# Two triangular inversions, issued as one block or step by step beside TensorE's main stream

## The chip, the cores and the metric

The kernel runs on one NeuronCore of a Trainium2 chip. The metric is the time of one execution on the device, in microseconds (us). Five engines take part: TensorE (PE: matrix products and transposes), VectorE (DVE), ScalarE (ACT), GpSimd (POOL) and SyncE (SP), whose queue issues nearly all the transfers of this kernel. Each engine runs its own list of instructions in order; semaphores make one engine wait for another.

## The reference

One step of a small hybrid decoder with an even and an odd layer, for a prompt of 2048 rows and 8 sample rows. The even layer has differential attention (4 heads) and a gated delta rule (4 heads) side by side. The change concerns the delta rule, which works in chunks:

```
M  = where(strict, (kb @ k^T) * decay, 0)
Tm = triangular_solve(eye + M, eye)          # the inverse of a unit lower triangle
u  = Tm @ (v * beta);  w = Tm @ (kb * exp(g))
# then, chunk by chunk, with the state S:
v_new = u - w @ S
o     = qg @ S + attn @ v_new
S     = S * gl + kg^T @ v_new
```

Every chunk of every head needs its `Tm` before the state can pass through it.

## The kernel before

The prompt is worked in two halves of 1024 rows (8 blocks of 128). All matrices of the projections are split into a high and a low part, and each product is made of three (`mm3`, lines 392 to 400).

**The parts of a half.** `a_group` (head by head) projects query, key and value of attention; `b_group` projects the delta rule's inputs, and `stage_a` behind it builds the chunk matrices and stores each chunk's strict triangle `N` in DRAM (`gn_d`); `z_group` projects the gates, `zt`, evacuated by ScalarE (tanh) and VectorE (a fused multiply and add that reads PSUM) from two PSUM buffers (line 508 on). `scan` runs the recurrence over 8 chunks; for each, `merge` reads the inverted diagonal blocks from DRAM (16 small loads a chunk, lines 741 and 742) and puts them together to the inverse of the whole chunk.

**The inversion.** `inverse` (lines 681 to 701) inverts the 32x32 diagonal blocks of all chunks and heads of a half: 128 blocks, one on each partition. It loads them with four transfers (`ivN`, line 687), sets `X` to the unit matrix, and goes over 31 rows, last to first. For a row with m entries right of the diagonal it multiplies (`ivp`, m x m products, `X` read transposed) and sums (`ivX`, a reduction to m values). Each row needs the row before it. In half 0 both instructions are on VectorE; in half 1 the 20 larger products (`r < IP`) are on GpSimd. At the end `X` and its transpose are stored (lines 698 and 701) for `merge`.

**What sets the order.** The Python functions are generators that trace instructions. `drive(main, *sides)` traces the main stream piece by piece, counts the TensorE time of each piece (its columns / 2400 us) on a clock, and traces one step of a side stream (`Side(gen, gap)`) whenever the clock has passed its due time, which then moves on by `gap`. `drain` traces what is left of a side stream; `run` traces a generator to its end. The traced order is not the final one: the kernel is built with `schedule_with_timeline_sim=True` (line 1920), by which a planner lays out each engine's list ahead of time with assumed durations, taking among the instructions whose operands are there by then the one traced first. `after` adds an order between two instructions; a `Side` with a window (`WS0A`, `WT0A`) uses it so that the main stream's products don't get too far ahead of the side's.

**Around the change.** In half 0 the last gates (`zb`, four `z_group` columns) are traced at lines 1720 to 1724, the last of them by `run(zb)`. The next lines traced are those of half 1: first `inverse(gp, 0)` and the first four gate columns of half 0 (lines 1699 and 1700), then `scan` of half 0 as a side stream (line 1701), `build_hT` (the normed input rows of half 1) and `a_group(…, 1, 0)`. In half 1, the first 16 of 64 pieces of `zb` are traced at line 1721; then come `inverse(gp, 1)` (line 1726), the other 48 pieces with attention of half 0 as a side stream `at` (lines 1734 and 1735), `a_group(…, 1, 1)`, and from there on `scan` of half 1 (line 1738) as a second side stream. Attention loads keys (`kl`), values, queries (`ql`) and, at each change of head, a row of biases (`biasR`), which VectorE turns round (`biasT`).

Of the kernel before, what the change touches and what calls it, by code (L numbers as in the profile page):

```python
# [33 lines left out]
SK = 6  # L34
KM = 3
CT = 0
WARM = 16
IP = 20
PC = (0,)
# [75 lines left out]
def hybrid_step_kernel(  # L115
# [209 lines left out]
    def run(*gens):  # L325
        for g in gens:
            for _ in g:
                pass
# [33 lines left out]
    def drive(main, *sides):  # L362
        n, m = len(PE.log), len(DVE.log)
        pace = []
        for t in main:
            clock[0] += t or 0.0
            if len(DVE.log) > m:
                pace.append(DVE.log[-1])
            for s in sides:
                if s.win and len(s.pe) >= s.win:  # L370
                    after(PE.log[n:], s.pe[-s.win])
            for s in sides:
                while not s.done and clock[0] >= s.due:
                    k = len(DVE.log)
                    s.step(pace)
                    if not s.vwin and len(DVE.log) > k:
                        pace.append(DVE.log[-1])
            n, m = len(PE.log), len(DVE.log)
# [139 lines left out]
    def z_group(st, wp, hs, half, idx):  # L518
        ws = [load_cols(wp, wic[i]) for i in idx]
        for part in range(2):  # L520
            for i, w in zip(idx, ws):
                ev = z_evac(st, i, half, part)
                for off, n in PARTS[half][part][2]:
                    ps = psD.tile([P, 512], F32, tag="d", name="psz")
                    yield from mm_cols(ps[:, :n], w, hs, part, off, n)
                    ev(ps[:, :n], off, n)
# [154 lines left out]
    def inverse(gp, half):  # L681
        N = gp.tile([P, 32, 32], F32, tag="pka", bufs=1, name="ivN")
        X = gp.tile([P, 32, 32], F32, tag="pkb", bufs=1, name="ivX")
        pr = gp.tile([P, 1024], F32, tag="ww", bufs=1, name="ivp")
        base = gn_d.offset + half * NB * H * P * P
        for b in range(4):
            SP.dma_start(N[32 * b:32 * b + 32],
                         bass.AP(tensor=gn_d.tensor, offset=base + 32 * b * P + 32 * b,
                                 ap=[[P * P, 32], [P, 32], [1, 32]]))
        DVE.memset(X, 0.0)  # L690
        DVE.memset(X.rearrange("p r c -> p (r c)")[:, ::33], 1.0)
        for r in range(30, -1, -1):
            m = 31 - r
            pv = pr[:, :m * m].rearrange("p (c s) -> p c s", s=m)
            tt(pv, bc(N[:, r:r + 1, r + 1:], [P, m, m]),
               X[:, r + 1:, r + 1:].rearrange("p s c -> p c s"), ALU.mult, POOL if half == 1 and r < IP else None)
            DVE.tensor_reduce(X[:, r, r + 1:], pv, axis=AX.X, op=ALU.add, negate=True)
        SP.dma_start(xb_d[half].rearrange("b u r c -> (b u) (r c)"), X.rearrange("p r c -> p (r c)"))
        prx = pr.rearrange("p (c r) -> p c r", r=32)
        DVE.tensor_copy(prx, X.rearrange("p r c -> p c r"))  # L700
        SP.dma_start(xbt_d[half].rearrange("b u r c -> (b u) (r c)"), pr)
# [977 lines left out]
    with ExitStack() as e1:  # L1679
        wp = (e1.enter_context(tc.tile_pool(name="wp", bufs=4)), 3)  # L1680
        st = e1.enter_context(tc.tile_pool(name="st", bufs=2))
        gsm = e1.enter_context(tc.tile_pool(name="gsm", bufs=2))
        with ExitStack() as eg:
            gp = eg.enter_context(tc.tile_pool(name="gp", bufs=1, side="right"))
            zt = []
            for i in range(6):
                z = gp.tile([P, H, P], F32, tag=f"zt{i}", name=f"zt{i}")
                DVE.memset(z, 0.0)
                zt.append(z)
            S = [gp.tile([P, H, P], F32, tag="S", bufs=2, name="S")]  # L1690
            DVE.memset(S[0], 0.0)
            psG0 = eg.enter_context(ExitStack())
            psG = psG0.enter_context(tc.tile_pool(name="psG0", bufs=3, space=PSUM, side="right"))
            gs = []
            for half in range(2):
                with tc.tile_pool(name=f"bh{half}", bufs=2, side="right") as bp, \
                        tc.tile_pool(name=f"psB{half}", bufs=2, space=PSUM, side="right") as psB:
                    if half == 1:
                        inverse(gp, 0)
                        run(z_group(st, wp, hs, 0, range(0, 2)), z_group(st, wp, hs, 0, range(2, 4)))  # L1700
                        sc = Side(scan(gp, psG, 0, gs[0], S, zt), GS0A, WS0A)
                    hs, build = build_hT(bp, psB, half)
                    ab = gsm.tile([P, NB, 8], F32, tag="ab", name="ab")
                    drive(a_group(st, wp, hs, half, 0, ab, build), *([sc] if half else []))
                with tc.tile_pool(name=f"sa{half}", bufs=1, side="right") as sa, \
                        tc.tile_pool(name=f"psA{half}", bufs=3, space=PSUM, side="right") as psA:
                    g = {}
                    gs.append(g)
                    pend = [gates(sa, psA, half, ab, gsm, g)]
                    sd = [Side(pump(pend), GA)] + ([sc] if half else [])  # L1710
                    if half == 0:
                        for h in range(1, H):
                            drive(a_group(st, wp, hs, half, h, None), *sd)
                    if half == 1:
                        sc.pace(GS0B, WS0B)
                    for h in range(H):
                        drive(b_group(st, wp, sa, psA, hs, half, h, g, pend), *sd)
                    if half == 1:
                        drain(sc)
                    zb = chain(z_group(st, wp, hs, half, range(4, 6)), z_group(st, wp, hs, half, range(6, 8)))  # L1720
                    drive(islice(zb, ZB), *sd)
                    flush(pend)
                    if half == 0:
                        run(zb)
            psG0.close()
            inverse(gp, 1)
            with tc.tile_pool(name="psG1", bufs=2, space=PSUM, side="right") as psG:
                with tc.tile_pool(name="atl0", bufs=1, side="right") as al, \
                        tc.tile_pool(name="atz0", bufs=1, side="right") as az, \
                        tc.tile_pool(name="ate0", bufs=1, side="right") as ae, \  # L1730
                        tc.tile_pool(name="psS0", bufs=2, space=PSUM, side="right") as psS, \
                        tc.tile_pool(name="psX0", bufs=1, space=PSUM, side="right") as psX, \
                        tc.tile_pool(name="psO0", bufs=1, space=PSUM, side="right") as psO:
                    at = Side(attention(split_tags(ae, al, az), psS, psX, psO, psX, "x", 0, 3), GT0A, WT0A)
                    drive(zb, at)
                    at.pace(GT0B, WT0B)
                    drive(a_group(st, wp, hs, 1, 1, None), at)
                    sc = Side(scan(gp, psG, 1, gs[1], S, zt), GS1C, WS1)
                    at.pace(GT0C, WT0C)
                    for h in range(2, H):  # L1740
                        drive(a_group(st, wp, hs, 1, h, None), at, sc)
                    zg = chain(z_group(st, wp, hs, 1, range(0, 2)), z_group(st, wp, hs, 1, range(2, 4)))
                    at.pace(GT0D, WT0D)
                    sc.pace(GS1D, WS1)
                    drive(islice(zg, ZH), at, sc)
                    drain(at, sc)
                SP.dma_start(gdn_p, S[0])
                pr = psG.tile([P, 512], F32, tag="g", name="prh")
                PE.transpose(pr[:36, :P], hist.rearrange("p g j -> p (g j)"), ident)
                hr = gp.tile([36, P], F32, tag="rr", bufs=1, name="hr")  # L1750
                DVE.tensor_copy(hr, pr[:36, :P])
                for gi in range(12):
                    SP.dma_start(gconv_p[0, 0, :, gi * P:gi * P + P], hr[gi * 3:gi * 3 + 3])
            hold(zg, HB0, RB0, at)
# [9 lines left out]
    with ExitStack() as e3, ExitStack() as eS:  # L1764
        wp = (e3.enter_context(tc.tile_pool(name="wp2", bufs=4)), 1)
# [158 lines left out]
```

## Time and profile before

| | |
|---|---|
| median of three runs | 2559.68 us (2556.47 to 2561.66) |
| profiled execution | 2560.37 us, of which the span from the first to the last instruction is 2558.7 |
| mean granted clock of TensorE | 0.981 |
| busy: PE | 2459.0 us (96%) |
| busy: DVE | 1752.6 us (68%) |
| busy: ACT | 1123.4 us (44%) |
| busy: POOL | 785.2 us (31%) |
| chain of work that ended last | PE 74%, DVE 10%, DMA 6%, ACT 3%, issue 3%, POOL 3% |

In rows of instructions the columns are: start, duration, engine, line, operation, output<-inputs, shapes, count, and in brackets the idle time of the engine before it and what ended it. Nearly all instructions have line 131 (the helper that records them), so they are told apart by the names of their tiles. In rows of stretches, busy times and numbers of instructions (x) follow for each engine, then the granted clock of TensorE as a share of full speed, the mean share of the DMA engines and GB/s.

### The profile page before, as it was taken

The numbers are of one execution on the slowest core, as the hardware profiler recorded it, in microseconds if no ns is written. First come the engines' busy times: TensorE is split into PE (matmuls) and PEld (weight loads), VectorE is DVE, ScalarE is ACT, GpSimd is POOL, SyncE is SP. The second block draws the span as 40 slices with busy tenths as digits, with TensorE's granted clock in tenths as the row PEclk, the third lists the DMA queues.
The fourth block names the chain that finished last, engine by engine and source line by source line (L and its number), as shares of the span: only waits on it lengthen the run. The fifth ranks groups of instructions, "written<-read, shape, count | busy, mean of one in ns | idle before, by whom it ended". The sixth has DMA issues, their size and how long they took to land.

```text
span 2558.7 us, 42320 instructions
## 1 busy us (share of the span) xinstructions
PE 2459.0 (96%) x14717; PEld 2164.2 (85%) x14717; DVE 1752.6 (68%) x4133; ACT 1123.4 (44%) x3129; POOL 785.2 (31%) x883
## 2 busy tenths in 40 slices
PE   9999999999998999989899899999999998999998
PEld 8989888988887999878778677788877788999986
DVE  7347766677778677667667878988866457666652
ACT  6445542655544566445543234344444353233220
POOL 3221110211125222101113767644311025555410
PEclk9999999999999999989999999999999999999999
DMA  4334464455453454465334544434354661221252
GB/s 160 112 113 125 127 169 124 131 158 151 140 160 106 122 157 119 122 208 180 109 108 152 171 126 145 149 114 142 114 165 150 214 199 32 75 67 51 73 162 73
DMA packets 262554, 337.45 MB, mean 132 GB/s; under 512 B 62842, under 2 KB 179068, under 8 KB 262332
## 3 DMA queue, kind: packets, MB, share of 16 engines
q1 hardware_dynamic: 252100, 301.18, 38.8%
q0 software_dynamic: 10240, 33.56, 4.5%
q8 instruction: 116, 1.90, 0.3%
q14 instruction: 98, 0.80, 0.1%
HBM read 246.99 MB, written 87.79 MB: 131 GB/s over the span
## 4 chain that ended last, share of the span: by engine, by line
PE 74%; DVE 10%; DMA 6%; ACT 3%; issue 3%; POOL 3%; SPq 0%; ACTq 0%; POOLq 0%; DVEq 0%
PE psp L131 13%; PE psw L131 12%; PE psa L131 10%; PE pso L131 8%; PE psb L131 8%; PE psz L131 4%; PE po L131 4%; PE s L131 3%; PE psy L131 2%; PE px L131 2%; DVE p L131 1%; DVE nm L131 1%; DVE wlo L131 1%; DMA E<-gr_d 1%; DMA wraw<-in_w_out_even_dram 1%
## 5 line engine op out<-in xcount | busy, mean ns | idle before, releaser
L926 ACT ACTIVATE p<-s,nm 128x512 f32<-128x512 f32 (+3 forms) x320 | 199.0, 625 | 293.4 <-DVE nm L131 255.6
L954 POOL TENSOR_SCALAR p<-p,gf 128x512 f32<-128x512 f32 (+3 forms) x160 | 123.0, 782 | 364.6 <-DVE gf L131 221.0
L131 PE MATMUL psp<-whi,ah 128*128 128x512 f32 (+1 forms) x544 | 217.4, 401 | 5.9 <-DVE xres L131 3.0
L131 PE MATMUL pso<-hhi,whi 128*128 128x512 f32 x512 | 208.2, 407 | 2.4 <-DVE ot L131 0.8
L131 PE MATMUL pso<-hhi,wlo 128*128 128x512 f32 x512 | 205.2, 401 | 0.0
L131 PE MATMUL pso<-hlo,whi 128*128 128x512 f32 x512 | 205.1, 401 | 0.0
L131 PE MATMUL psp<-wlo,ah 128*128 128x512 f32 x512 | 204.2, 399 | 0.5 <-DVE wlo L131 0.5
L131 PE MATMUL psp<-whi,al 128*128 128x512 f32 x512 | 203.1, 397 | 0.0
L131 DVE TENSOR_TENSOR wlo<-wraw,whi 128x1024 fp32r<-128x1024 f32 (+2 forms) x128 | 151.3, 1185 | 66.0 <-ACT whi L313 64.2
L313 ACT CAST whi<-wraw 128x1024 fp32r<-128x1024 f32 (+2 forms) x136 | 135.1, 998 | 135.4 <-PE psz L131 29.9
L131 PE MATMUL psa<-whi,hhi 128*128 128x384 f32 (+1 forms) x544 | 190.5, 351 | 1.5 <-ACT hhi L283 1.5
L131 PE MATMUL psa<-wlo,hhi 128*128 128x384 f32 (+1 forms) x544 | 186.2, 342 | 1.4 <-DVE wlo L131 1.3
L131 PE MATMUL psa<-whi,hlo 128*128 128x384 f32 (+1 forms) x544 | 187.3, 344 | 0.0
L131 PE MATMUL psb<-hhi,whi 128*128 128x512 f32 (+1 forms) x480 | 175.9, 367 | 2.4 <-ACT xc L587 2.4
L131 PE MATMUL psb<-hhi,wlo 128*128 128x512 f32 (+1 forms) x480 | 168.7, 352 | 0.0
L131 PE MATMUL psb<-hlo,whi 128*128 128x512 f32 (+1 forms) x480 | 168.0, 350 | 0.0
L131 DVE TENSOR_REDUCE nm<-s 128x1 f32<-128x512 f32 (+3 forms) x256 | 147.3, 587 | 19.7 <-PE s L131 18.4
L131 PE MATMUL po<-v,at 128*128 128x128 f32 x1088 | 157.3, 282 | 0.7 <-ACT at L963 0.7
L131 PEld LDWEIGHTS po<-v,at 128*128 128x128 f32 x1088 | 147.4, 198 | 8.1 <-ACT at L963 1.9
L131 PE MATMUL s<-kst,QH 128*128 128x512 f32 (+3 forms) x320 | 126.4, 406 | 26.8 <-ACT p L926 26.3
L131 DVE SCALAR_TENSOR_TENSOR p<-p,gf 128x512 f32<-128x512 f32 (+3 forms) x160 | 130.8, 840 | 13.7 <-POOL p L954 13.4
L131 DVE TENSOR_TENSOR xres<-xres,psp 128x512 f32<-128x512 f32 (+1 forms) x68 | 46.6, 685 | 123.1 <-PE psp L131 96.8
(413 smaller groups left out, 6923.9 us busy)
## 6 DMA issues: line engine op xcount, KB each, us to landing
wraw<-in_w_in_even_c_dram SPq DMA_DIRECT2D x40, 512.0 KB
asrc<-og_d SPq DMA_DIRECT2D x32, 512.0 KB
wraw<-in_w_in_odd_dram SPq DMA_DIRECT2D x32, 512.0 KB
wr<-in_w_in_odd_dram SPq DMA_DIRECT2D x32, 512.0 KB
wraw<-in_w_in_even_a_dram SPq DMA_DIRECT2D x24, 384.0 KB
xrow<-in_x_prompt_dram SPq DMA_DIRECT2D x16, 512.0 KB
qd_d<-qn SPq DMA_DIRECT2D x64, 128.0 KB
gu_d<-cv SPq DMA_DIRECT2D x32, 256.0 KB
```

What stands on the lines that cost most here:

```text
L131: r = f(*a, **k)
L313: ACT.copy(hi, raw)
L926: ACT.activation(p[:, e, :w], s[:, :w], AF.Exp, bias=nm, accum_out=b["sums"][:, e, c:c + 1])
L954: POOL.tensor_scalar(p[:, 1, :w], p[:, 1, :w], gf[:, 1, c:c + 1], 1.0, ALU.mult, ALU.mult)
```

## The change

`inverse` yields after its setup and after every row. In half 0 it becomes a side stream with a step of 1.3 us of the main stream's clock beside the four gate columns that were traced behind it; what is left is drained before the scan is set up. In half 1 it becomes a side stream with a step of 1.6 us beside the rest of `zb` and beside `a_group(…, 1, 1)`, behind attention in each round, and is drained before the second scan is set up.

```
+GIV0 = 1.3
+GIV1 = 1.6
...
         DVE.memset(X.rearrange("p r c -> p (r c)")[:, ::33], 1.0)
+        yield
         for r in range(30, -1, -1):
             m = 31 - r
             pv = pr[:, :m * m].rearrange("p (c s) -> p c s", s=m)
             tt(pv, bc(N[:, r:r + 1, r + 1:], [P, m, m]),
                X[:, r + 1:, r + 1:].rearrange("p s c -> p c s"), ALU.mult, POOL if half == 1 and r < IP else None)
             DVE.tensor_reduce(X[:, r, r + 1:], pv, axis=AX.X, op=ALU.add, negate=True)
+            yield
...
                     if half == 1:
-                        inverse(gp, 0)
-                        run(z_group(st, wp, hs, 0, range(0, 2)), z_group(st, wp, hs, 0, range(2, 4)))
+                        iv = Side(inverse(gp, 0), GIV0)
+                        drive(chain(z_group(st, wp, hs, 0, range(0, 2)), z_group(st, wp, hs, 0, range(2, 4))), iv)
+                        drain(iv)
                         sc = Side(scan(gp, psG, 0, gs[0], S, zt), GS0A, WS0A)
...
-            inverse(gp, 1)
+            iv = Side(inverse(gp, 1), GIV1)
...
                     at = Side(attention(split_tags(ae, al, az), psS, psX, psO, psX, "x", 0, 3), GT0A, WT0A)
-                    drive(zb, at)
+                    drive(zb, at, iv)
                     at.pace(GT0B, WT0B)
-                    drive(a_group(st, wp, hs, 1, 1, None), at)
+                    drive(a_group(st, wp, hs, 1, 1, None), at, iv)
+                    drain(iv)
                     sc = Side(scan(gp, psG, 1, gs[1], S, zt), GS1C, WS1)
```

## Rows read from the trace of the kernel before

**Rows 1.** Busy time of each engine in six stretches, all instructions.
```profile
358.00:417.00 59.00, 52.70 (x326) 47.15 (x326) 54.29 (x85) 13.56 (x25) 2.38 (x6) 0.97 0.46 140
417.00:741.00 324.00, 323.95 (x1969) 284.23 (x1968) 215.06 (x541) 167.71 (x527) 47.28 (x76) 1.00 0.52 148
741.00:811.00 70.00, 61.95 (x317) 52.72 (x316) 61.07 (x155) 27.84 (x96) 42.08 (x36) 0.95 0.38 117
835.00:850.00 15.00, 12.16 (x72) 11.48 (x72) 7.75 (x25) 6.14 (x22) 1.58 (x3) 0.77 0.51 129
850.00:1080.00 230.00, 226.89 (x1552) 211.00 (x1553) 162.76 (x562) 132.48 (x522) 58.45 (x87) 1.00 0.46 133
```

**Rows 2.** The same for instructions on `ivX` alone: VectorE, GpSimd, clock.
```profile
358.00:417.00 59.00, 40.93 (x63) 0.00 (x0) 0.97 0.46 140
741.00:811.00 70.00, 19.29 (x43) 32.36 (x20) 0.95 0.38 117
```

**Rows 3.** Timelines of SP, TensorE and ScalarE: work ahead of its traced place.
```profile
356.59 0.36 SPq L428 DMA_DIRECT2D xrow<-in_x_prompt_dram  x1
...
444.42 0.34 PE L131 MATMUL psa<-whi,hhi 128*128 128x392 f32 x1
...
714.85 0.40 PE L131 MATMUL psz<-hhi,whi 128*128 128x512 f32 x1
...
818.85 1.08 PE L131 MATMUL psz<-zt,zt 128*128 128x64 f32 x8 [0.42 <-DMA zt<-xbt_d]
...
853.61 0.48 ACT L497 COPY qkv<-psa 128x384 f32<-128x384 f32 x1 [0.20 <-PE psa L131]
```

**Rows 4.** TensorE's waits, 358 to 417 us (total, times, longest); two on its timeline.
```profile
PE psz L131 <- DVE zt L131: 6.2, 5, 1.9
...
408.03 0.39 PE L131 MATMUL psz<-hhi,whi 128*128 128x260 f32 x1 [0.54 <-DVE zt L131]
415.48 0.39 PE L131 MATMUL psz<-hhi,whi 128*128 128x260 f32 x1 [1.11 <-DVE zt L131]
```

**Rows 5.** Timelines of ScalarE (first two rows) and VectorE around the fifth wait.
```profile
393.32 1.05 ACT L313 CAST whi<-wraw 128x1024 fp32r<-128x1024 f32 x1 [5.76 <-PE psz L131]
...
411.87 0.38 ACT L509 ACTIVATE zt<-psz 128x260 f32<-128x260 f32 x1
...
411.08 1.94 DVE L131 TENSOR_TENSOR ivp<-ivN,ivX 128x961 f32<-128x961 f32 x1
...
415.01 0.42 DVE L131 SCALAR_TENSOR_TENSOR zt<-zt,psz 128x260 f32<-128x260 f32 x1
```

**Rows 6.** TensorE's timeline, 741 to 811 us: four of its waits.
```profile
759.94 0.41 PE L131 MATMUL pqT<-ident,ql 128*128 128x128 f32 x2 [1.38 <-issue]
...
771.18 0.50 PE L131 MATMUL s<-kst,QH 128*128 128x512 f32 x1 [0.78 <-ACT p L926]
...
773.39 0.41 PE L131 MATMUL px<-ident,p 128*128 128x128 f32 x2 [0.91 <-DVE p L131]
...
796.45 0.58 PE L131 MATMUL s<-kst,QH 128*128 128x256 f32 x1 [2.63 <-ACT p L926]
```

**Rows 7.** Timelines of VectorE (two rows) and GpSimd: work beside a product of the inversion.
```profile
786.97 2.38 DVE L131 SCALAR_TENSOR_TENSOR qn<-qkv,rs,qkw 128x128 f32<-128x128 f32 x1 [0.20 <-POOL rs L189]
789.34 0.34 DVE L131 SCALAR_TENSOR_TENSOR qn<-qkv,rs,qkw 128x128 f32<-128x128 f32 x1
...
786.90 2.30 POOL L173 TENSOR_TENSOR ivp<-ivN,ivX 128x784 f32<-128x784 f32 x1
```

**Rows 8.** SP's queue before the second inversion.
```profile
734.62 0.93 SPq L687 DMA_DIRECT2D ivN<-gn_d  x2
```

**Rows 9.** Timelines of SP, VectorE and TensorE, 830 to 841 us.
```profile
836.11 0.42 SPq L845 DMA_DIRECT2D biasR<-bv_d  x1
...
839.93 0.29 DVE L131 COPY biasT<-biasR 128x256 f32<-128x256 f32 x1 [3.32 <-DMA biasR<-bv_d]
...
840.61 1.97 PE L131 MATMUL psz<-zt,zt 128*128 128x64 f32 x8 [2.84 <-DVE zt L131]
```

## The prediction

> **What bounds the kernel now.** I read the page first, then cut the span into stretches by what VectorE does for the two inversions, then asked what TensorE waited for inside them. Between the inversions, from 417 to 741 us, TensorE is busy 323.95 of 324 us at full granted clock, with VectorE at two thirds [rows 1]: TensorE's own work sets the time there. In the two stretches with an inversion it is not so. From 358 to 417 us TensorE lacks 6.3 us (59 - 52.70) and the clock stands at 0.97, which is another 1.8 us of work not done (0.03 x 59); from 741 to 811 us it lacks 8.05 us and, at 0.95, another 3.5 us [rows 1]. Together 19.6 us, 0.8% of the span, lie where the edit works. VectorE is busy 54.29 of 59 us and 61.07 of 70 us there [rows 1], of which the inversion takes 40.93 and 19.29 us; the second one also takes 32.36 us of GpSimd [rows 2]. A third loss stands just behind the second inversion: 2.84 us and, at 0.77, 3.45 us of clock from 835 to 850 us [rows 1]. So the question is which of these losses follow from where the inversion's instructions rank, and which from their being there at all.
>
> **What the change does to the instructions.** It adds none and removes none: the same 31 products and 31 sums per half, the same memsets, copy, four loads and two stores. What moves is their place in the traced order. Before, all of an inversion is traced in one block; after, one row (a product and a sum) is traced for every 1.3 us (half 0) or 1.6 us (half 1) of TensorE work that the main stream counts. Half 0: the main stream behind it counts 4 x 24 x (512 + 260 + 260) / 2400 = 41.3 us, so about 32 of 33 steps are set among it and `drain` traces the rest. Half 1: 48 pieces of 0.64 us and 64 of 0.48 us are 61.4 us, and 33 steps need 52.8.
>
> The first thing to settle is what a later place is worth. The trace says: it is a rank, not a date. The input rows of half 1, traced behind all of `z_group(0..3)`, are fetched at 356.59 us, 88 us before the first product of the `a_group` they belong to, at 444.42 [rows 3]. The second scan, traced behind `a_group(1, 1)`, has its first product at 818.85 us, while that group's eighth and last block is copied out only at 853.61 [rows 3]. An instruction whose operands are there is put into any gap. An inversion row needs only the row before it, so a lower rank will not make it wait for its step; it only lets a `zt`, `wlo` or attention instruction pass that is ready at the same moment.
>
> **Half 0, step by step.** TensorE's waits there are five, 6.2 us, all for the evacuation `zt` on VectorE [rows 4]. Which of them can a rank cure? The cast of the last weight of `z_group(2..3)` needs the slot of the last column of the rest of `zb`, and runs at 393.32 us [rows 5]; so what TensorE does before that is `zb`, which line 1724 traces ahead of the inversion in both kernels. The first three waits, 6.2 - 0.54 - 1.11 = 4.6 us, and what they cost of the 1.8 us of clock, lie there with ranks unchanged. Left are the waits that end at 408.03 and 415.48, 0.54 + 1.11 = 1.65 us [rows 4]. At the second, ScalarE had done its half of `zt` by 411.87 + 0.38 = 412.25; VectorE was in a product until 413.02 and did its own half at 415.01 [rows 5]. Passing what stands between (the last row's sum, a `wlo`) would bring it forward by up to 2.0 us, enough to end the wait of 1.11. But VectorE has little slack (54.29 of 59 us [rows 1]): what passes the inversion pushes the inversion, and the next `zt` stands behind a product of up to 1.94 us [rows 5] again. Bounds 0 and 1.65 us; I take 1.0, nearer to the upper, since the rows show the passing to be possible in both cases.
>
> **Half 1, step by step.** Here the inversion is traced ahead of everything, so its ranks do fall. TensorE's waits from 741 to 811 us sum to 8.0. Three of them, 0.78 + 0.91 + 2.63 = 4.3 us [rows 6], trace back to a VectorE instruction held up beside a GpSimd product of the inversion. `qn` takes 2.38 us from 786.97 where the next one takes 0.34; a product runs on GpSimd from 786.90 for 2.30, and both end within 0.2 us of each other [rows 7]. The 20 GpSimd products stay, so some VectorE instruction will be beside each of them whatever the ranks; I take none of the 4.3 us. The remaining 3.7 us (1.38 of it at 759.94 [rows 6]) end in chains of attention through VectorE in which sums of the inversion (19.29 us in 70 [rows 2]) stand; half of that, 1.8 us. Of the 3.5 us of clock I take a third, 1.1, since the longest wait, 2.63 us, is the likeliest to have brought the clock down, and it stays. Sum 2.9 us, bounds 0 and 11.5, and below nothing by up to 2.6 if one more hold-up of the size of the one at 796.45 arises.
>
> The Trainium skill (SBUF — State Buffer, Who interferes with whom) says that a VectorE instruction with two SBUF inputs and a GpSimd instruction that reads SBUF cannot run together, and that the second to start blocks until the first ends. The pair above agrees with it. By that rule the 4.3 us stay and the sum below is 3.9 us; were the long VectorE instructions a mere backlog that rank cures, it would be 4.3 + 2.4 of clock more, 10.6 us.
>
> **The queues.** On SP the four loads of `ivN` are issued from 734.62 on, two in 0.93 us [rows 8], so some 2 us in all, ahead of attention's first loads; after, they rank behind these, which by the same price, six or seven loads, are some 3 us of issue in turn. The inversion starts about 3 us later, attention's products about 2 us sooner. TensorE waits for neither: it has no wait in this stretch before the one that ends at 759.94 [rows 6], because the rest of `zb` keeps it busy. So I cost it at nothing; without that cover the price would be those 2 to 3 us. GpSimd: attention's `p` and the reciprocal roots now pass the products; each gains at most one product, up to 3 us, and the inversion's end moves later, by my estimate from before 811 (all its 43 VectorE and 20 GpSimd instructions lie ahead of that [rows 2]) to between 812 and 825 us. Who waits for that end is the second scan: its trace position is behind `a_group(1, 1)`, which lasts to 853.61 [rows 3], and its first product at 818.85 is 35 us ahead of that, so there is room.
>
> **The jam at 835 us.** SP stood in the second scan's merge loads before it could issue attention's `biasR` at 836.11; VectorE then stood 3.32 us at `biasT`, with the scan's evacuation behind it, and TensorE 2.84 [rows 9]; with the clock, 6.3 us in all [rows 1]. A later end of the inversion moves the merges against attention's change of head. Value 0, bounds 6.3 us either way.
>
> **Sum.** 1.0 + 2.9 + 0 = 3.9 us off the profiled execution's 2560.4 us (span 2558.7), 2556.5. The median of the three runs is 0.7 us below that execution, so 2555.8 us for the median.
>
> **Rivals.**
> Held to its steps: if a lower rank does spread the second inversion to where its last step is traced (`zb` and `a_group(1, 1)` count 41.0 + 30.7 = 71.7 us and run from 714.85 to 853.61 [rows 3]; the last step stands at 10.2 + 52.8 = 63.0 of these, so at about 837 us), VectorE's share falls and TensorE runs as it does from 850 to 1080, where it lacks 1.4% [rows 1], 1.0 us in 70. Then 8.05 + 3.5 - 1.0 = 10.6 us return, the jam's 6.3 may be missed by the later merges, and half 0 gives 1.0: up to 17.9, likely some 16 us, 2543.7 us. For it: the losses stand nowhere but at the inversions. Against it: [rows 3]. The Trainium skill (Perfetto Trace Analysis, Optimization Strategy) holds that a kernel with several regimes may gain by interleaving them; that would be this case.
> More jam (the slower side): the merge loads of chunks 0 and 1, 16 each, come behind the inversion's stores. If the inversion ends past about 822 us, they are issued across attention's change of head, and a second stand like [rows 9] arises: + 6.3 us and no gain, 2566.0. If it ends past 836, the head's loads are ahead and the jam is gone.
> Nothing moves: the gaps were filled the same way before, since an inversion instruction can follow its predecessor only when that is finished and others slip in there; 2559.7 us.
>
> **How the numbers follow.** The forecast, 2555.8 us, has chance 0.48 (own range 2550 to 2563); held to its steps 0.22; more jam 0.18; nothing moves 0.12. A measurement of this kernel tells about 0.2%, 5.1 us, from no change. Faster by over that: 0.18 of the forecast's 0.48, all 0.22 of the first rival, none of the others: 0.40. Slower: 0.15 of the jam's share, 0.02 each of the forecast's and the last one's: 0.19. Within: 0.41. The range 2541 to 2567 reaches to both far cases and leaves out the deepest gains of the first rival and a jam that costs more than it did.
>
> **What would show it.** In the profile after: first inversion still over within 3 us of 417, with at least three waits for `zt` before 393 us; second inversion over between 812 and 825; VectorE instructions still held beside GpSimd products; TensorE lacking 5 us or more between 741 and 811. If the inversion's sums stand evenly up to about 837 us or beyond and TensorE lacks under 2 us there, my reading of rank was wrong and the first rival holds. If merges and a late `biasR` show a stand of over 3 us twice, it is the jam.

## The result, and the profile after

| | before | after |
|---|---|---|
| median | 2559.53 us of 6 (2556.47 to 2562.17) | 2574.21 us of 6 (2571.51 to 2580.86) |
| ratio | | 1.0059, 95% interval 1.0046 to 1.0072 |
| profiled execution, its span | 2558.7 us | 2572.4 us |
| busy: PE, DVE, POOL | 2459.0, 1752.6, 785.2 us | 2463.5, 1756.6, 776.2 us |

The change costs 14.7 us. The forecast was 2555.8 us with a range of 2541 to 2567; it was wrong in sign, and the time lies 7 us above the range.

Busy time by stretch in the kernel after; columns as in [rows 1] (PE, PEld, DVE, ACT, POOL, then TensorE's granted clock, DMA share, GB/s):

```profile
358.00:417.00 59.00, 53.84 (x326) 48.44 (x325) 54.28 (x85) 13.31 (x24) 2.23 (x6) 0.94 0.46 142
417.00:741.00 324.00, 324.00 (x1970) 284.51 (x1969) 215.01 (x542) 167.84 (x527) 47.18 (x76) 1.00 0.52 148
741.00:811.00 70.00, 56.97 (x275) 48.32 (x274) 58.15 (x143) 25.43 (x84) 36.82 (x32) 0.90 0.34 97
...
811.00:861.00 50.00, 48.25 (x308) 45.67 (x306) 33.95 (x106) 26.37 (x102) 12.73 (x20) 0.93 0.46 131
...
835.00:850.00 15.00, 13.82 (x101) 12.88 (x99) 10.38 (x35) 6.73 (x22) 2.94 (x5) 1.00 0.48 129
...
1310.00:1560.00 250.00, 235.47 (x1175) 192.73 (x1174) 179.93 (x410) 81.95 (x196) 133.63 (x121) 0.97 0.45 139
1560.00:1710.00 150.00, 134.62 (x688) 111.51 (x687) 130.62 (x319) 57.22 (x138) 84.89 (x79) 0.94 0.47 140
```

The same for the kernel before, where [rows 1] does not have the stretch:

```profile
811.00:861.00 50.00, 46.24 (x304) 43.73 (x303) 31.21 (x106) 27.55 (x100) 10.21 (x16) 0.93 0.44 118
...
1310.00:1560.00 250.00, 233.20 (x1163) 191.80 (x1163) 188.79 (x414) 79.45 (x194) 135.38 (x122) 0.96 0.46 138
1560.00:1710.00 150.00, 145.69 (x783) 121.11 (x782) 130.42 (x350) 65.44 (x156) 91.24 (x82) 1.00 0.48 148
```

Two stretches have become worse. From 741 to 811 us, where the second inversion runs, TensorE lacks 13.0 us of 70 at a clock of 0.90, against 8.05 us at 0.95 before [rows 1]. And from 1560 to 1710 us, 750 us behind the end of the second inversion, it lacks 15.4 us of 150 at 0.94, against 4.3 us at 1.00. The second is the larger: 11.1 us of waits and 9 us of clock (0.06 x 150).

To follow the loss along the kernel I take from each trace when the same instructions run (evacuations and casts of weights, in order), subtract their time in the kernel before, and take the median of the seven nearest each point. This is the **lag** in us; + is later. Each lag is read from the one profiled execution of a run, which can lie up to 7 us from the run's median (e6: 2576.55 against 2583.82). Kernels with the same early order lie at most 2.7 us apart up to 1071 us.

| kernel | 741 | 811 | 861 | 1071 | 1562 | 1600 | 1705 | end |
|---|---|---|---|---|---|---|---|---|
| after | -0.4 | +6.2 | +4.5 | +4.8 | -6.3 | +6.1 | +13.6 | +13.8 |

So the change loses 5 us at the inversion, wins 11 us from 1071 to 1562 us (6 of them by 1310, ahead of the odd layer) and loses 20 us between 1562 and 1705 us, most of it in one place (12.4 us by 1600). Here are TensorE, VectorE and GpSimd around it in the kernel after, then VectorE and GpSimd at the same point in the kernel before (timelines; columns as in front, a bracket is idle time and what ended it):

```profile
1579.70 1.09 PE L133 MATMUL px<-ident,p 128*128 128x128 f32 x4 [7.48 <-DVE p L133]
...
1571.42 1.04 DVE L133 TENSOR_TENSOR skt<-skt,sqb 128x512 f32<-128x512 f32 x1 [2.33 <-DMA sqb<-qs_d]
1572.38 7.18 DVE L133 SCALAR_TENSOR_TENSOR p<-p,gf 128x512 f32<-128x512 f32 x1
...
1569.87 3.03 POOL L958 TENSOR_SCALAR p<-p,gf 128x512 f32<-128x512 f32 x4
1572.88 6.13 POOL L175 TENSOR_TENSOR skt<-skt,sqb 128x512 f32<-128x512 f32 x5
```

```profile
1567.84 1.27 DVE L131 SCALAR_TENSOR_TENSOR p<-p,gf 128x512 f32<-128x512 f32 x2
...
1573.88 0.69 DVE L131 TENSOR_TENSOR skt<-skt,sqb 128x512 f32<-128x512 f32 x1 [0.54 <-DMA sqb<-qs_d]
...
1573.92 5.53 POOL L173 TENSOR_TENSOR skt<-skt,sqb 128x512 f32<-128x512 f32 x4 [0.59 <-DMA sqb<-qs_d]
```

`skt` is a page of the sample's key cache, `sqb` the sample's query row. Each page is multiplied by the row; of every four such products GpSimd has three. Each new row has to land first, and then GpSimd does the products of all pages that are waiting in one run. That run stands in the kernel before as well (5.53 us at 1573.92). The difference is attention's `p` (its weights, scaled by `gf`): before, the four `p` of this block were laid out ahead of VectorE's own product with the new row and were done at 1569.1; after, the first of them stands behind it, with VectorE waiting 2.33 us for the transfer; it starts at 1572.38, half a microsecond ahead of GpSimd's run and beside GpSimd's last own `p`, and takes 7.18 us where a `p` takes 0.6. It is **held**: what it needs of GpSimd, the first of the four `p` in the row of 1569.87, is done before it starts. TensorE waits 7.48 us for it. Nothing of this is in the diff.

### The profile page after: what moved, and what is told of

The parts are those of the page before. It is cut to its first block, busy times and chain, and to the rows that moved or that the text cites. A ratio compares the mean times of both kernels' runs of the same rounds, so it can differ in the third digit from the quotient of the medians.

```text
span 2572.4 us, 42339 instructions
## 1 busy us (share of the span) xinstructions
PE 2463.5 (96%) x14717; PEld 2166.0 (84%) x14717; DVE 1756.6 (68%) x4133; ACT 1121.1 (44%) x3129; POOL 776.2 (30%) x883
## 5 line engine op out<-in xcount | busy, mean ns | idle before, releaser
L133 DVE SCALAR_TENSOR_TENSOR p<-p,gf 128x512 f32<-128x512 f32 (+3 forms) x160 | 134.6, 863 | 15.9 <-POOL p L958 15.5
L967 ACT COPY at<-px 128x512 f32<-128x512 f32 (+3 forms) x160 | 82.2, 521 | 107.3 <-PE px L133 106.9
```

The costliest lines, as they stand in the source:

```text
L133: r = f(*a, **k)
L967: ACT.copy(at[:, :nblk], px[:, :nblk])
```

## The experiments

Two questions: what in the change moves the lists (the orders in which the planner lays out each engine's instructions) at all, and whether the late loss belongs to the change. Theory A: only one rank matters, that of the second inversion's set-up against attention's first step. Its rival B: spreading the rows costs. Theory C: the odd layer's order is laid out anew for any small shift, as in a draw of lots, and its time with it. Its rival D: the changed kernel lost there by something that it did.

| run | what | median us | ratio to before | lag 811 | 861 | 1071 | 1562 | 1705 |
|---|---|---|---|---|---|---|---|---|
| e1 | set-up first | 2560.66 | 0.9997 (0.9988 to 1.0007) | -1.0 | -0.8 | -0.8 | -2.1 | -0.8 |
| e2 | attention's step first | 2576.85 | 1.0050 (1.0033 to 1.0067) | +8.7 | +3.1 | +3.0 | -2.5 | +16.6 |
| e3 | bias, keys first | 2561.11 | 0.9993 (0.9982 to 1.0004) | +1.2 | -0.3 | -0.2 | -0.5 | -0.8 |
| e4 | queries first | 2565.36 | 1.0007 (0.9997 to 1.0016) | +4.5 | -0.4 | -0.0 | -10.6 | +1.4 |
| e5 | before, pace 1.79 | 2575.54 | 1.0056 (1.0039 to 1.0073) | +0.2 | -1.0 | -1.0 | -5.7 | +9.0 |
| e6 | after, pace 1.79 | 2583.82 | 1.0096 (1.0079 to 1.0113) | +6.2 | +4.7 | +4.7 | -4.4 | +11.0 |
| e7 | before, pace 1.85 | 2559.06 | 0.9996 (0.9984 to 1.0007) | +1.0 | +0.3 | +0.2 | -1.5 | -0.1 |
| e8 | after, pace 1.85 | 2569.00 | 1.0025 (1.0013 to 1.0038) | +6.2 | +4.7 | +4.7 | +13.2 | +15.6 |
| e9 | before, skt on DVE | 2569.44 | 1.0035 (1.0023 to 1.0046) | +0.0 | -1.4 | -1.3 | -9.2 | +6.1 |
| e10 | after, skt on DVE | 2559.37 | 0.9996 (0.9984 to 1.0008) | +7.1 | +5.8 | +5.6 | -10.1 | +3.2 |
| e11 | before, two rows | 2568.05 | 1.0026 (1.0015 to 1.0037) | +1.3 | +0.1 | +0.4 | +5.7 | +11.5 |
| e12 | after, two rows | 2575.41 | 1.0057 (1.0041 to 1.0074) | +8.2 | +3.1 | +3.1 | +6.9 | +14.4 |
| e13 | before, inversion on DVE | 2580.07 | 1.0068 (1.0051 to 1.0085) | +12.3 | +5.0 | +11.1 | +11.6 | +13.4 |
| e14 | after, inversion on DVE | 2573.14 | 1.0037 (1.0023 to 1.0051) | +13.6 | +6.9 | +6.9 | +1.1 | +13.9 |
| e15 | after, pace binds, 1.6 | 2564.87 | 1.0009 (0.9999 to 1.0019) | -10.4 | -17.4 | +1.6 | +4.5 | +5.9 |
| e16 | before, single skt | 2578.35 | 1.0058 (1.0041 to 1.0075) | +0.4 | +1.0 | +1.0 | -2.2 | +19.2 |
| e17 | after, pace binds, 1.0 | 2576.69 | 1.0055 (1.0039 to 1.0072) | -6.5 | -1.3 | +6.8 | +4.5 | +16.3 |
| e18 | before, skt on DVE, 1.85 | 2585.33 | 1.0106 (1.0089 to 1.0123) | -0.4 | -0.5 | -0.4 | +0.7 | +14.4 |

### One rank: e1 to e4

e1, in the kernel after:

```
+                    next(iv.gen)
                     drive(zb, at, iv)
```

> Both side streams stay as in the changed kernel, paced at 1.3 and 1.6; only the set-up of the second inversion (four loads, two memsets) is traced ahead of the attention's first step again. Theory A (one rank): the pace of the streams reaches no list, and all of the lost time hangs on that one set-up standing behind the attention's first step; the lists of TensorE, VectorE, ScalarE and GpSimd come out as in the kernel before, and the time is 2559.5 us, within 3 us, with the second inversion's last sum at 807 us. Theory B (spreading): the inversion's rows dealt out between TensorE's products are what costs: 2574 us, last sum at 813 us.

2560.66 us, last sum at 805.7 us. Theory A. Tracing the four loads and two memsets ahead of attention's first step takes the whole loss away, with both streams still paced. The lists themselves say the same. In the traces VectorE, ScalarE and GpSimd have the same instructions in the same order in e1 as in the kernel before. In the built programs TensorE has too, and only eight of SP's places differ, stores and merge loads of half 0. And the changed kernel, built with 0.8, 1.0 or 2.5 us in place of 1.6 for the second stream, has the same lists on all engines.

e2, in the kernel before:

```
         qload(*items[1])
+        if half == 0:
+            yield 0.0
...
-            inverse(gp, 1)
...
                     at = Side(attention(...), GT0A, WT0A)
+                    for _ in range(1):
+                        next(at.gen)
+                    inverse(gp, 1)
                     drive(zb, at)
```

> No side stream at all: the kernel before, with the attention's first step (loads of keys, bias and two queries, the first query's transposes) traced ahead of the whole second inversion. Theory A (one rank): the same 2574 us as the changed kernel, within 3 us, though nothing is paced. Theory B (spreading): 2559.5 us, as before.

2576.85 us. Theory A again, from the other side: no stream, no pace, and the loss is there, with the same 12 us between 1562 and 1600 us (lag -2.5, then +9.2). The lists of the four compute engines are those of the changed kernel. e1 and e2 together show what makes the changed kernel's lists: one rank.

e3 and e4 are e2 with that `yield` further ahead in the first step (in e4 behind the queries, with keys and bias moved behind it), so that only `kload` and `bias`, or only `qload` and `query`, are ahead of the inversion.

> As the run before, but only the loads of the keys and the bias and the copy of the bias are traced ahead of the inversion; the query loads stay behind it. If VectorE's copy of the bias ahead of its other work, or the keys' load ahead of the inversion's loads, is what costs: 5 us lost by 1071 us, and 2564 us or more. If it is the queries: nothing lost by 1071 us, 2559.5 us within 3.

Nothing lost, 2561.11 us. VectorE's copy of the bias ahead of its other work is harmless.

> The counterpart: only the two query loads and the first query's transposes are traced ahead of the inversion; keys and bias stay behind it. If the queries are the cause: 4 to 7 us lost by 1071 us, as in the changed kernel (4.8), while the end may lie anywhere from 2550 to 2580 us, since the odd layer from 1310 us is laid out anew. If bias and keys are the cause: nothing lost by 1071 us.

A miss in part: 4.5 us are lost by 811 us, but they are won back by 861, in the stretch in which the kernel before has its jam [rows 9]. So neither part alone costs what both cost together (3.0 to 5.6 us at 1071 us in six kernels with the attention step ahead). The odd layer of e4 is another draw: 10.6 us ahead at 1562 us, and lost again by 1600, where its `p` takes 6.58 us at 1567.76.

### A draw: e5 to e8

```
-GMA = 1.8
-GMB = 1.8
+GMA = 1.79      # e5, e6; 1.85 in e7, e8
+GMB = 1.79
```

> The kernel before, with the two paces of the sample stream in the odd layer (from about 1300 us) 1.79 in place of 1.8. Nothing of the inversions is touched. Theory C (a draw): the odd layer's order is laid out anew for any small shift, and how many of the sample's GpSimd products meet a VectorE operation on TensorE's path is luck; the time moves by more than the measurement's 3 us, to anywhere in 2550 to 2580 us, with nothing lost by 1300 us. Theory D (the layer is robust, and the changed kernel lost there by something that it did): 2560 us, within 3.

> The changed kernel with the same paces, 1.79. The planner lays its lists from about 1560 us on as in the run before, though not those of 741 to 851 and of 1136 to 1560 us. Theory C: the loss of 20 us between 1562 and 1705 us isn't there, or is in both of the pair; the pair differs by the early part alone, -6 to +6 us. Theory D: 14 us behind its partner, as the changed kernel was.

> As the 1.79 run of the kernel before, with 1.85. Theory C: another draw, anywhere in 2550 to 2580 us. Theory D: 2560 us, within 3.

> The changed kernel with 1.85; its lists from about 1540 us on are those of its partner. Theory C: -6 to +6 us against its partner, with the early +5 at 1071 us as in the changed kernel. Theory D: 14 us behind it.

e5 is the run that tells most of the late loss. The kernel before, its inversions untouched, its lag within 3 us up to 1310 us, loses 16 us between 1562 and 1600 us (-5.7 to +10.5) and ends at 2575.54 us, where the changed kernel ended. In its timelines the same pair of engines stands there:

```profile
1572.44 0.79 PE L131 MATMUL s<-kst,QH 128*128 128x512 f32 x1 [8.46 <-ACT p L926]
...
1566.03 5.58 DVE L131 SCALAR_TENSOR_TENSOR nm<-mx,nm 128x1 f32<-128x1 f32 x1
...
1566.68 4.91 POOL L173 TENSOR_TENSOR skt<-skt,sqb 128x512 f32<-128x512 f32 x4
```

Here it is `nm`, one number per partition, that takes 5.58 us beside four products (in e6 an `ocv`, 7.35 us at 1566.27, beside five). With 1.85 the kernel before has one wait of 5.4 us there, at 1544 us, and stays at 2559.06 us. So 0.01 us in a pace is worth 15 us, and the odd layer's time follows from which instruction meets which run.

The medians of the pairs alone settle nothing: they lie 8.3 and 9.9 us apart, between the 6 us of theory C and the 14 of theory D, and theory C's number failed. What speaks against D is where the time goes. From about 1580 us on the lists of VectorE, ScalarE and GpSimd are the same in both kernels of each of these pairs, and from 1562 to 1705 us, where the changed kernel lost 20 us, both lose alike: 14.7 and 15.4 us in e5 and e6, 1.4 and 2.4 in e7 and e8 (lag 1705 less lag 1562). The later pair e11 and e12 does the same, 5.8 and 7.5. So theory D is out: the late loss goes with the order, whichever kernel has it.

What separates the pairs is not one thing. The 4.5 to 5.7 us that the changed kernel lies behind at 1071 us do not simply stay: e6 is 0.6 us behind e5 at 1310 us, and in the profiled executions 0.7 us at the end (spans 2574.9 and 2574.2). That was the shortest of e6's four times, which reach to 2590.86; no trace shows where the longer ones lose. e8 is 6.7 us behind e7 at 1310 us and 14.7 at 1562; the lists of a pair differ from 1131 us on.

### What the draw is made of: e9 to e12, e16, e18

e9, e10 and e18 set `KM = 0` (no key product of the sample on GpSimd; e18 with the pace 1.85), e16 sets `KM = 1`, e11 and e12 give `sqb` two buffers:

```
-KM = 3
+KM = 0
...
-            qb = sp.tile([P, 512], F32, tag="sqb", bufs=1, name="sqb")
+            qb = sp.tile([P, 512], F32, tag="sqb", bufs=2, name="sqb")
```

> The kernel before, with the sample's 48 key products that GpSimd had (skt<-skt,sqb) all on VectorE: some 48 x 0.69 = 33 us of work more for VectorE between 1300 and 1560 us, and no product there for it to be held beside. If VectorE's being held beside GpSimd's products is what rules this stretch (theory C), the held time of 1310 to 1530 us (21 us in the kernel before) falls to under 5, and TensorE's wait for a held p goes; the time may still rise or fall by 10 us, by VectorE's added work against the 21 us.

> The changed kernel with the same products on VectorE. Theory C: the 7.5 us wait of TensorE for a held p at 1580 us is gone, the held time of 1530 to 1710 us (20 us in the changed kernel) falls under 8, and the pair differs by -5 to +5 us. Theory D: the changed kernel stays 14 us behind its partner.

For the held time I count, of each VectorE instruction over 0.5 us longer than the lower quartile of its form, the excess. From 1530 to 1710 us it is 6.7 us before, 15.9 after; from 1310 to 1530 us 17.7 and 13.0. With another lower bound the sums move by up to 4 us (the expectations have 21 and 20), so only large differences are read from them. In e9 it falls to 0.0 (1310 to 1530) and 4.0 (1530 to 1710), in e10 to 3.5 and 3.8, and TensorE's wait at 1580 is gone. So that wait was VectorE held beside those products: shown. But the pair ends 10 us apart, not within 5, the changed kernel ahead, and each has a new wait near 1630 us (e9):

```profile
1631.65 0.80 PE L131 MATMUL s<-kst,QH 128*128 128x512 f32 x1 [5.12 <-ACT p L926]
```

> The kernel before, with two buffers in place of one for the sample's query row (sqb), so that the row's load no longer waits for the last product of the batch before, and the products need not come in a burst of four or five when the row lands. Theory C: fewer and shorter holds (no hold of VectorE over 4 us from 1310 to 1710 us), and 0 to 10 us won. Against it: bursts come of the pages' loads and not of the row, and nothing changes but the draw.

> The changed kernel with two buffers for the query row; from about 1555 us on its lists are its partner's. Theory C: no 7 us hold at 1580 us, and -6 to +6 us against its partner. Theory D: 14 us behind it.

With the row loaded ahead there is no 7 us hold at 1580 us, as expected, but the held time of 1310 to 1530 us in e11 is 22.0 us, no less than the 17.7 before, TensorE has waits of 2.5 to 4.3 us elsewhere, and both are slower than the kernel before. The gain did not come, and the pair is 7.4 us apart, not within 6.

> The kernel before with one of four of the sample's key products on GpSimd in place of three of four, so that they no longer stand there in runs of three. If the long holds come of such runs: no hold of VectorE over 3 us beside skt products from 1310 to 1600 us, held time of 1310 to 1530 us under 10 us (21.2 in the kernel before), and 0 to 10 us won by 1530 us; VectorE has 32 x 0.69 = 22 us more to do, which may take that back. If not: held time as before.

Half a miss. No instruction is held for over 3 us any more (2.8 is the longest), so the long holds do come of runs. But the held time of 1310 to 1530 us falls only to 12.1 us, and TensorE has a wait of 9.02 us at 1520 us, again for a `p` behind a product with a new row (VectorE's product there waited 1.61 us for `sqb`). So single products on GpSimd don't take the long waits of TensorE away.

> The kernel before with all the sample's key products on VectorE, as in the run e9, and the sample's first two paces 1.85 in place of 1.8. If GpSimd's products are the one source of the late scatter: 2569 us as with 1.8, within 4. If the order by itself makes the draw, through whatever wait then comes last: more than 4 us away from that, between 2550 and 2575 us; below 2555 us it would beat both kernels.

2585.33 us, 16 us from e9 and above the range given: with no key product on GpSimd the pace still draws. GpSimd's runs are one of the ways in which the draw costs time, not its source.

### The early loss: e13, e14

```
-IP = 20
+IP = 0
```

> The kernel before with all 31 products of the second inversion on VectorE: its 20 large ones leave GpSimd (9910 elements a partition at 2.0 ns, some 20 us of VectorE in place of the 12.3 us for which it was held there). Lost or won by 861 us: -5 to +8 us. The held time of 741 to 815 us falls from 12.3 to under 4 us.

> The changed kernel with the same products on VectorE. If its early loss is VectorE's waiting for and being held beside GpSimd's products: it lies within 2 us of its partner at 861 and 1071 us (the changed kernel lay 4.6 behind), and TensorE's waits at 761 and 803 us are gone. If the earlier attention loads cost by themselves: still 4 to 6 us behind its partner there.

Without GpSimd's products no VectorE instruction is held for over 0.5 us from 741 to 815 us (0.0 us in e13 and e14, against 11.6 in the kernel before and 14.7 in the changed one), and the pair is 1.9 us apart at 861 us. At 1071 us it is not within 2 us: there the changed kernel is 4.2 us ahead of its partner. But TensorE's long wait near 761 us stands in both (3.5 and 4.6 us), and both lose 5 us and more, since VectorE now has the products to do. So the runs don't settle it; what the rows of the kernel after show is a queue. `pqT` needs the buffer that VectorE's last `kst` reads, and that stands behind the inversion's sums, which wait for products, and a held `gf`. A second `p` and GpSimd's product of 841 elements make the other long wait (TensorE, VectorE, GpSimd):

```profile
761.42 0.41 PE L133 MATMUL pqT<-ident,ql 128*128 128x128 f32 x2 [3.46 <-issue]
...
802.93 0.93 PE L133 MATMUL ptO<-ident,o 128*128 128x128 f32 x4 [2.90 <-DVE o L133]
...
755.42 0.39 DVE L133 TENSOR_REDUCE ivX<-ivp 128x15 f32<-128x225 f32 x1 [0.91 <-POOL ivp L175]
...
759.58 1.01 DVE L133 TENSOR_TENSOR gf<-gf,lam 128x1 f32<-128x1 f32 x1
760.62 0.69 DVE L133 TENSOR_TENSOR kst<-pkT,kst 64x512 fp32r<-64x512 f32 x1
...
798.58 3.26 DVE L133 SCALAR_TENSOR_TENSOR p<-p,gf 128x512 f32<-128x512 f32 x2
...
798.60 2.42 POOL L175 TENSOR_TENSOR ivp<-ivN,ivX 128x841 f32<-128x841 f32 x1
```

At 761 us the wait is 2.1 us longer than the one of [rows 6], at 803 us 2.5 us longer than before (0.43). That this is all of the early loss is argued, not shown.

### A pace that binds: e15, e17

```
-            iv = Side(inverse(gp, 1), GIV1)
+            iv = Side(inverse(gp, 1), GIV1, 0, 1)
```

> The changed kernel with the second inversion's rows tied to VectorE's order: each row's VectorE instructions may not be laid out ahead of the last one that the main stream had issued, as the sample stream's are already. So the pace of 1.6 us reaches the lists. If spreading the inversion is worth what the change is for: 3 to 8 us won by 861 us against the changed kernel, and 0 to 3 against the kernel before. If the inversion is limited by its own chain of products and sums (70 us in the kernel before): nothing won, and its last sum comes after 815 us, with the merge behind it late: 0 to 10 us lost by 861 us against the changed kernel.

> As the run in which the pace binds, with the pace of the second inversion 1.0 in place of 1.6 us. If the pace was only too slow: last sum at about 830 us (859 at 1.6, 807 before), the scan no longer late, and 2 to 8 us ahead of the kernel before at 1071 us; the end is then that less or more the odd layer's draw, 2548 to 2575 us. If the loss is only shifted: within 2 us of the kernel before at 1071 us, as at 1.6.

e15, 741 to 811 and 811 to 861 us:

```profile
741.00:811.00 70.00, 68.53 (x385) 61.42 (x384) 52.52 (x173) 35.19 (x127) 23.88 (x33) 1.00 0.41 113
811.00:861.00 50.00, 36.01 (x192) 32.73 (x190) 46.07 (x103) 24.08 (x91) 30.99 (x25) 0.86 0.36 107
```

A step that reaches the lists does what the first rival priced: TensorE lacks 1.5 us of 70 at full clock, and the main stream is 10.4 us ahead at 811 us and 17.4 at 861. But the last sum comes at 858.8 us (806.7 before), VectorE is busy 46.07 of 50 us in the stretch behind, TensorE lacks 14.0 us there, and at 1071 us nothing is left (+1.6). With 1.0 the last sum comes at 839.6 us, TensorE lacks 14.5 us from 811 to 861, and the lag at 1071 is +6.8. My "pace only too slow" is out. "Only shifted, within 2 us of the kernel before at 1071 us" fits e15, but not e17, which is 6.8 us behind. That the 52 us of VectorE and GpSimd work of this inversion [rows 2] have to be paid ahead of the scan at any pace is how I read both; it is argued, not shown.

No run is measurably faster than the kernel before.

## Why the prediction was wrong, by its steps

Two steps failed: in half 1 the queue was priced at nothing, and behind the edit nothing was priced at all.

**Rank, not date: right, and more than I took it for.** The input rows and the scan's early products [rows 3] were the right rows. The pace reaches no list: e1 and the built programs show it.

**Half 0: value 0, not 1.0.** The lists of the compute engines are the same ones in this stretch, so the `zt` that I saw able to pass did not: here rank reached nothing either. The waits are 5.1 us in four (6.2 in five [rows 4]), which with the same lists is no work of ranks; the one of 1.11 us stands as 1.13 at 415.17. TensorE takes 1.1 us longer for the same 326 instructions, at a clock of 0.94 against 0.97. Why the planner left it in its place no run shows.

**Half 1: the step that failed first.** I took 2.9 us won, at worst 2.6 lost; 6.6 us were lost by 811 us (lag -0.4 to +6.2). The price of the queue went in at nothing. I had the mechanism (loads of `ivN` behind attention's loads, inversion later, attention earlier) and the price without cover, 2 to 3 us, and then found cover in a single place: TensorE's first wait. The inversion did start 2.3 us later (first product at 743.57 us against 741.29); SP and VectorE in the kernel after:

```profile
735.03 0.42 SPq L882 DMA_DIRECT2D ql<-qd_d  x1
735.51 1.30 SPq L689 DMA_DIRECT2D ivN<-gn_d  x2
737.83 0.54 SPq L882 DMA_DIRECT2D ql<-qd_d  x1
738.42 1.04 SPq L689 DMA_DIRECT2D ivN<-gn_d  x2
...
743.57 0.16 DVE L133 TENSOR_TENSOR ivp<-ivN,ivX 128x1 f32<-128x1 f32 x1 [4.30 <-DMA ivN<-gn_d]
```

The cover was real until 758 us, where TensorE's wait of 3.46 us begins. But the shift had set VectorE's later order, sums against `kst`, `p` and `gf`, and that, as far as the rows show it, was paid at 761 and 803 us. The 4.3 us of holds stayed, as I took it. The 1.1 us of clock went the other way: the granted clock fell from 0.95 to 0.90, 3.5 us more of work not done.

**The jam: right as an unknown, and it went the good way.** From 835 to 850 us TensorE is busy 13.82 us at full clock; before 12.16 at 0.77 [rows 1], that is 1.7 + 3.45 = 5.1 us less lost. VectorE still stands 2.81 us at `biasT` (at 844.29 us, by its timeline), but TensorE has no wait over 0.33 us in that stretch. The rival "more jam" had 2566.0 us, the nearest number, by a mechanism that did not occur.

**The list of signs held but for one and proved little.** First inversion's last sum done at 413.9 us and its copy at 416.1; the second's last sum at 813.9, in the 812 to 825 foretold; VectorE held beside products; 13 us lacking from 741 to 811. Of three waits for `zt` before 393 us only two stand, at 361.50 and 388.74 us. All of it looked at the stretches of the edit.

**The missing term.** No part of the sum, the rivals or the range had the 750 us behind the edit, where the order of the odd layer was laid out anew: the lists come together at about 850 us, and part again from 1131 to about 1955 us. From 1071 us on the changed kernel won 11 us and lost 20. The kernels with the inversions of the kernel before and a small change in the sample stream (e5, e7, e9, e11, e16, e18) spread from 2559.1 to 2585.3 us. A range from local bounds alone could not hold that; by these six it should have reached some 25 us above.

How much of the 14.7 us is the early loss can't be read off. At 1071 us it is 4.8 us (3.0 to 5.6 in the six kernels that have its early order), and that much is the change's own. But the lists part again behind that, and by 1310 us the lag is -1.1. From 1136 to 1310 us, before and after:

```profile
1136.00:1310.00 174.00, 158.47 (x843) 130.07 (x841) 124.25 (x260) 99.76 (x224) 32.77 (x44) 0.98 0.47 154
...
1136.00:1310.00 174.00, 160.37 (x859) 130.26 (x858) 126.25 (x260) 99.40 (x226) 30.07 (x44) 1.00 0.49 157
```

So all of what was lost at the end came behind 1310 us, by the draw. With the four other pairs, after less before is +14.7, +8.3, +9.9, -10.1 and +7.4 us (and -6.9 in e14 against e13, with the inversion on VectorE). The sizes are those of the draw, and what the change costs apart from it five pairs do not settle.

## What to carry to other kernels

Where a planner lays out the lists, first ask of an edit which instruction passes which: a side stream whose rows depend on each other is bound by its own chain, and its pace may reach no list at all. Then price the stages far behind the edit too: small changes that touch nothing of it (a pace by 0.01 us) measure how far the time moves by order alone, and a gain or loss under that size can't be put down to the edit by its time alone. A wait that is spread out of one stretch has to be followed to where the work is needed; the 10 us won at the inversion in e15 were lost again by 1071 us.

## What the hardware showed

A VectorE instruction that meets a back-to-back run of GpSimd instructions can be held through the whole run, and need not be. In the kernel after `p` was held through the end of GpSimd's own `p` and all five products behind it, 7.18 us; in e5 an `nm` of one element per partition was held through four, 5.58 us. But in the kernel before two VectorE instructions were done in the middle of a run of five (VectorE, GpSimd):

```profile
1545.26 1.67 DVE L131 TENSOR_TENSOR skt<-skt,sqb 128x512 f32<-128x512 f32 x1
...
1547.99 1.85 DVE L131 SCALAR_TENSOR_TENSOR ocv<-ocg,cols,ocv 128x512 f32<-128x512 f32 x1
...
1545.10 7.10 POOL L173 TENSOR_TENSOR skt<-skt,sqb 128x512 f32<-128x512 f32 x5 [0.87 <-DMA sqb<-qs_d]
```

Each took about 1 us longer than it takes alone (0.7 us), and that run took 7.10 us where the five products after took 6.13. The prediction's rule from the Trainium skill (SBUF — State Buffer, Who interferes with whom) has the second to start blocked until the first ends. The two instructions in the middle, held for about one product each, agree with it; `p` and `nm` went on being blocked when the first had ended and the next product began. What decides between the two no run here shows. So an operation of any size can cost the whole run, but it is not certain to.
